# Which modulation chunks GpSimd sums in a two-layer mixer and MoE trunk, and when its residual rows are scaled

## Chip, cores and metric

The kernel runs on one core of a Trainium2 chip. The metric is the device time of one launch in microseconds. The kernel before takes 720.09 us, the median of three runs (717.9, 720.09 and 725.78).

## What is computed

The reference is a trunk of two layers on 256 tokens of width 1024. Each layer modulates its input with six vectors that come from one condition vector `c`, runs three token mixers (attention on selected keys, retention, mLSTM), and then a mixture of 16 experts of which two are taken for each token. Cut to what the change touches, it reads:

```python
c_act = silu(c)
for l in range(2):
    mod = c_act @ w_ada[l] + b_ada[l]            # w_ada[l]: 1024 x 6144
    sh_m, sc_m, g_m, sh_f, sc_f, g_f = split(mod, 6)
    h = x * (1 + sc_m) + sh_m
    mix = token_mixers(h, w_in[l], w_out[l], ...)   # key selection: top 64 of 256 scores
    x = layer_norm(ALPHA * x + (1 + g_m) * mix, ln_mix_g[l], ln_mix_b[l])
    h = x * (1 + sc_f) + sh_f
    y = moe_ffn(h, ...)
    x = layer_norm(ALPHA * x + (1 + g_f) * y, ln_ffn_g[l], ln_ffn_b[l])
```

## The kernel before

**Stages.** Each layer runs its mixers (the input projections in eight chunks, 0 to 7, then the output projection), then routing and the experts. Weights come through a ring of ten tiles of 512 KB that SyncE fills in the order of a written-out list; a tile is filled again when the engine that read it last is done. Every projection weight is split on chip into a high and a low part: ScalarE casts it (`A.copy` in `split`, L415), VectorE subtracts (L416), and TensorE multiplies three times (L434 to L436). So TensorE's projections are fed by ScalarE and VectorE, each of which takes its instructions in order.

**Modulation chunks.** `w_ada` is cut into 12 chunks of 512 columns for each layer, named (layer, chunk): 0 to 3 shift and scale of the mixers, 4 and 5 their gate, 6 to 9 shift and scale of the experts, 10 and 11 the experts' gate. A chunk is four tiles of the ring and is summed over 1024 rows in one of two ways:

- on TensorE (`ada`, L362, through `ada_half`, L349): 8 matmuls of 512 columns against the broadcast condition into PSUM, which the trace records as two passes each, a copy to SBUF (L364), then for a shift or scale four transposes (L404) and a small reduction on VectorE (L406), for a gate one summing matmul (L396). A gate's bias is added to the SBUF row by VectorE (L394), except where `ada_half` is told to add it by one more matmul (L353).
- on GpSimd (`ada_pool`, L370): ScalarE scales the eight half tiles by the condition (L210), GpSimd adds them up in seven additions of 128x512 (L380), and at the next call of `behind` TensorE sums over partitions with four one-column matmuls (L410).

`behind(n)` is called when the matmuls of projection chunk n have been written into the program. It first finishes chunks that GpSimd has summed, then starts those that the table `LATER` lists for n; `POOLED` names the ones that go to GpSimd.

**Key selection and softmax.** Scores of 256 keys (chunk 0's projection) go through eight rounds of MAX8 and MATCH_REPLACE on VectorE for each half of the tokens (L578 to L585) in the early part of each layer. The attention's softmax follows: VectorE masks and finds maxima (L623, L624), ScalarE takes the exponential, GpSimd multiplies by the reciprocal sums (L633), TensorE transposes (L636). The retention's rotation after chunk 5 uses GpSimd too (L528).

**Residual rows.** At the start of layer 1 the normalized rows `xn` (tile H) become the scaled residual `xres` (tile X) by eight GpSimd instructions (`affine_rows`, L463 and L464), for which two row tiles of 512 KB are loaded. The residual is used only after the output projection of the layer. In the convolution of the mLSTM a work tile `cvs` is taken from tag H.

The instructions of an engine stand in an order that a scheduler sets when the kernel is built, from the order of the code, its priorities and its waits.

## Time and profile before

| | |
|---|---|
| median of three runs | 720.09 us |
| the profiled execution | 720.78 us |
| its span, first to last instruction | 719.0 us |
| TensorE busy in it | 665.7 us (93%) |
| VectorE, ScalarE, GpSimd busy | 399.6, 281.2, 161.4 us |
| mean granted TensorE clock | 0.959 of 2.4 GHz |
| mixers of layer 0, then experts | 0 to about 217 us, 217 to 368 us |
| mixers of layer 1, then experts | 368 to about 556 us, 556 to 719 us |

The span is what the profiler saw between first and last instruction; the execution lasts 1.8 us longer. Busy shares are means over the whole span, so what a stage waits for is read from short windows of it: the busy time of each engine there, and beside it the granted clock, where 1.00 is 2.4 GHz and 0.50 is 1.2 GHz.

### The profile page before, as it was taken

How to read it: one execution, taken by the hardware profiler on the slowest of the kernel's cores; microseconds unless marked ns; L12 is line 12 of the kernel's file. 1: busy time of each engine (PE TensorE's matmuls, PEld its weight loads, DVE VectorE, ACT ScalarE, POOL GpSimd, SP SyncE). 2: the span in 40 equal slices, each digit the busy share in tenths (PEclk: the TensorE clock that was granted, in tenths of full speed). 3: DMA queues.
4: the chain of work that ended last, by engine and by line, in shares of the span. 5: the costliest groups of instructions: out<-in, count | busy, mean ns of one | idle time of the engine just before them, and what ended most of it. 6: DMA issues, size and time to landing. Idle time of an engine off the chain costs nothing. (4 is left out here: it accounts for less than half of the span.)

```text
span 719.0 us, 10379 instructions
## 1 busy us (share of the span) xinstructions
PE 665.7 (93%) x3638; PEld 410.1 (57%) x3638; DVE 399.6 (56%) x911; ACT 281.2 (39%) x583; POOL 161.4 (22%) x163
## 2 busy tenths in 40 slices
PE   5899799999998999989989999999999799999994
PEld 1567687865775433434338678894576644434431
DVE  5478987643765331244377999764547522234345
ACT  3346748344622222222246646853633221222231
POOL 3012943200003036120035513310000303612001
PEclk9999979999996999999997999999999699999998
DMA  8997773499996899999945773447998569999951
GB/s 305 407 377 240 253 261 96 145 342 410 411 359 252 288 322 364 357 406 410 383 142 183 242 244 114 138 153 253 402 326 257 194 237 326 347 350 407 406 190 58
DMA packets 57759, 204.18 MB, mean 284 GB/s; under 512 B 7336, under 2 KB 7464, under 8 KB 56422
## 3 DMA queue, kind: packets, MB, share of 16 engines
q1 hardware_dynamic: 55152, 198.49, 75.7%
q0 software_dynamic: 2112, 4.44, 1.6%
q8 instruction: 30, 0.49, 0.3%
q10 hardware_dynamic: 438, 0.54, 0.2%
q14 instruction: 27, 0.22, 0.1%
HBM read 202.15 MB, written 4.19 MB: 287 GB/s over the span
## 5 line engine op out<-in xcount | busy, mean ns | idle before, releaser
L416 DVE TENSOR_TENSOR sb_w<-sb_ring,sb_w 128x512 fp32r<-128x512 f32 (+1 forms) x156 | 109.8, 715 | 44.7 <-ACT sb_w L415 43.1
L415 ACT CAST sb_w<-sb_ring 128x512 fp32r<-128x512 f32 (+1 forms) x156 | 92.0, 608 | 82.4 <-PE ps_mm L435 49.1
L1205 PE MATMUL ps_s<-sb_ring,sb_S 128*64 128x512 f32 x424 | 113.8, 601 | 0.2 <-PEq L1114 0.2
L435 PE MATMUL ps_mm<-sb_w,sb_H 128*128 128x512 f32 (+2 forms) x224 | 80.7, 363 | 3.3 <-DVE sb_H L889 3.3
L434 PE MATMUL ps_mm<-sb_w,sb_H 128*128 128x512 f32 (+2 forms) x224 | 80.7, 368 | 2.4 <-ACT sb_w L415 1.7
L436 PE MATMUL ps_mm<-sb_w,sb_H 128*128 128x512 f32 (+2 forms) x224 | 75.6, 373 | 0.8 <-DVE sb_w L416 0.6
L1205 PEld LDWEIGHTS ps_s<-sb_ring,sb_S 128*64 128x64 f32 x424 | 32.3, 137 | 54.3 <-issue 48.1
L349 PE MATMUL ps_t<-sb_ring,cact 128*32 128x512 f32 x272 | 48.0, 621 | 7.2 <-DVE posf L296 6.2
L434 PEld LDWEIGHTS ps_mm<-sb_w,sb_H 128*128 128x128 f32 x224 | 43.7, 197 | 11.3 <-ACT sb_w L415 2.7
L435 PEld LDWEIGHTS ps_mm<-sb_w,sb_H 128*128 128x128 f32 x224 | 44.0, 197 | 9.1 <-DVE sb_H L889 4.0
L436 PEld LDWEIGHTS ps_mm<-sb_w,sb_H 128*128 128x128 f32 x224 | 42.3, 197 | 12.1 <-issue 3.8
L1104 DVE TENSOR_SCALAR sb_S<-ps_t,afffg,afffb 128x256 f32<-128x256 f32 x32 | 17.4, 543 | 51.7 <-ACT sb_S L210 51.7
L1096 PEld LDWEIGHTS ps_t<-sb_O,sb_H 128*128 128x128 f32 x256 | 33.1, 193 | 19.9 <-issue 12.2
L1253 PE MATMUL ps_t<-sb_P,sb_sg 128*64 128x512 f32 x152 | 42.0, 599 | 0.9 <-ACT sb_sg L1240 0.9
L210 ACT ACTIVATE sb_S<-ps_t,afffb,afffg 128x256 f32<-128x256 f32 x32 | 18.0, 563 | 59.1 <-PE ps_t L1096 59.0
L1096 PE MATMUL ps_t<-sb_O,sb_H 128*128 128x256 f32 x256 | 38.9, 297 | 2.0 <-DVE sb_O L1026 1.8
L435 PE MATMUL ps_mm<-sb_H,sb_w 128*128 128x256 f32 x128 | 38.1, 298 | 2.8 <-DVE sb_w L416 2.8
L434 PE MATMUL ps_mm<-sb_H,sb_w 128*128 128x256 f32 x128 | 37.9, 298 | 0.0
L436 PE MATMUL ps_mm<-sb_H,sb_w 128*128 128x256 f32 x128 | 37.9, 296 | 0.0
L1036 POOL MEMSET sb_X<- 128x2048 f32 x2 | 3.6, 1804 | 151.3 <-DVE sb_H L836 151.3
L633 POOL TENSOR_SCALAR sb_sg<-sb_sg,sm 128x128 f32<-128x128 f32 (+1 forms) x32 | 26.4, 842 | 47.1 <-DVE sm L630 24.9
L528 POOL TENSOR_TENSOR sb_rope<-sb_rope 128x256 f32<-128x256 f32 (+1 forms) x16 | 15.9, 992 | 89.1 <-DVE iwm L564 31.3
(369 smaller groups left out, 1214.2 us busy)
## 6 DMA issues: line engine op xcount, KB each, us to landing
sb_ring<-w_gu SPq DMA_DIRECT2D x106, 512.0 KB, 7.0
sb_ring<-w_ada SPq DMA_DIRECT2D x96, 512.0 KB, 7.1
sb_P<-w_dn SPq DMA_DIRECT2D x58, 512.0 KB, 9.7
sb_ring<-w_in SPq DMA_DIRECT2D x56, 512.0 KB, 6.0
sb_ring<-w_out SPq DMA_DIRECT2D x16, 512.0 KB, 10.1
sb_S<-w_gu SPq DMA_DIRECT2D x6, 1024.0 KB, 8.2
sb_row<-rows SPq DMA_DIRECT2D x8, 512.0 KB, 8.1
sb_w<-w_gu SPq DMA_DIRECT2D x12, 256.0 KB, 3.9
```

What stands on the lines that cost most here:

```text
L210: return A.activation(o, i, f, bias=bias, scale=scale)
L349: PE.matmul(pa[32 * g:32 * g + 32, :], cact[:, k:k + 1].to_broadcast([P, 32]), w[g // 2][:, (g % 2) * 512:(g % 2) * 512 + 512], start=(i = ...
L415: A.copy(hi, src)
L416: V.tensor_tensor(lo, src, hi.bitcast(F32), op=OP.subtract)
L434: PE.matmul(o, a[0], b[0], start=start, stop=False)
L435: PE.matmul(o, a[1], b[0], start=False, stop=False)
L436: return PE.matmul(o, a[0], b[1], start=False, stop=stop)
L633: G.tensor_scalar(sg[:, i * n:(i + 1) * n], sg[:, i * n:(i + 1) * n], sm[:, h:h + 1], None, op0=OP.mult)
L1096: last = PE.matmul(pt[:, j * 256:(j + 1) * 256], src[:, tt * D + k * P:tt * D + (k + 1) * P], oh[:, tt * D + q * 256:tt * D + (q + 1) * 25 ...
L1104: V.tensor_scalar(o, t, gp[:, k:k + 1], bp[:, k:k + 1], op0=OP.mult, op1=OP.add)
L1205: PE.matmul(pgu[s * 64:s * 64 + 64, :], xg[:, c0:c0 + 64], ws[s][k], start=(i == order[0] and k == 0), stop=(i == order[3] and k == 1), ti ...
L1253: PE.matmul(pyb[s * 64:s * 64 + 64, :], hdT[:, k, s * 64:s * 64 + 64], wd[s][k], start=(k == 0), stop=(k == 1), tile_position=(0, 64 * s))
```

## The change

Three things change together.

1. The tables. In layer 0, chunks (0,6) and (0,7), which GpSimd summed behind projection chunk 3, are summed on TensorE behind chunk 2; (0,5) moves from behind chunk 2 to behind chunk 1; (1,0) and (1,2), which TensorE summed behind chunk 6, are summed by GpSimd behind chunks 5 and 6. In layer 1, (1,6) and (1,7), which TensorE summed behind chunk 6, are summed by GpSimd behind chunks 5 and 6.
2. Gates that TensorE sums with `ada` get their bias by the extra matmul (L353): (0,4), (0,5) and (1,10).
3. The residual rows of layer 1 are scaled behind chunk 5, in place in `xn`, and issued after the last softmax multiplication of GpSimd, not at the layer's start; their loads move in the list from ahead of chunk 0 to ahead of chunk 6. The convolution's work tile is taken from tag X in layer 1.

In all, TensorE loses two chunks (16 matmuls of 512 columns and 8 transposes) and gets three bias matmuls and eight one-column matmuls more; GpSimd has 14 additions more; ScalarE has 16 scalings more and two copies fewer; VectorE loses three bias additions and two reductions.

```diff
@@ -48,11 +48,12 @@
 LATE_ROWS = (False, True)
 
 
-LATER = [{2: [(0, 5)], 6: [(0, 9), (1, 0), (1, 2)], 3: [(0, 6), (0, 7)], 5: [(0, 8)], 7: [(1, 3), (1, 1)], 1: [(0, 4)]}, {2: [(1, 5), (1, 8)], 6: [(1, 10), (1, 7), (1, 6)], 7: [(1, 9)]}]
+LATER = [{1: [(0, 4), (0, 5)], 2: [(0, 6), (0, 7)], 5: [(1, 0), (0, 8)], 6: [(1, 2), (0, 9)], 7: [(1, 3), (1, 1)]},
+         {2: [(1, 5), (1, 8)], 5: [(1, 6)], 6: [(1, 7), (1, 10)], 7: [(1, 9)]}]
 EARLY = [[], [(1, 4)]]
 LAST = [[(0, 10), (0, 11)], [(1, 11)]]
 
-POOLED = [(1, 5), (0, 6), (0, 7)]
+POOLED = [(1, 0), (1, 2), (1, 5), (1, 6), (1, 7)]
 
 SLOT = {"ring": 1024, "X": 2048, "H": 2048, "O": 2048, "S": 2048, "P": 1024,
         "w": 512, "rope": 512, "sg": 512, "e": 512, "a": 512, "h": 256, "g0": 1024, "g1": 1024, "row": 1024}
@@ -153,13 +154,13 @@
                     st.add(("in", l, n), chunk(l, n), which=(i,))
         for la, na in EARLY[l]:
             st.add(("ada", la, na), w_ada[la, na])
-        if l:
-            norm_rows(2 * l - 1)
         for n in range(8):
             if l or n > 1:
                 st.add(("in", l, n), chunk(l, n))
             for la, na in LATER[l].get(n, ()):
                 st.add(("ada", la, na), w_ada[la, na])
+            if l and n == 5:
+                norm_rows(2 * l - 1)
         norm_rows(2 * l)
         for n, which in ((0, (0, 1)), (1, (0, 1)), (0, (2,)), (1, (2,)), (0, (3,)), (1, (3,))):
             st.add(("out", l, n), w_out[l, n], which=which)
@@ -361,8 +362,9 @@
 
     def ada(l, n, tag="t"):
         a = sb("a")
-        (V.tensor_copy if n < 4 and l == 0 else A.copy)(a, ada_sums(l, n, tag))
-        modulation(l, n, a, quad, tag)
+        gate = n % 6 > 3
+        (V.tensor_copy if n < 4 and l == 0 else A.copy)(a, ada_sums(l, n, tag, gate))
+        modulation(l, n, a, quad, tag, gate)
 
     pending = []
 
@@ -505,6 +507,9 @@
             if l == 0 and n == 5:
                 with tc.issue_after(st.last.ins):
                     nc.sync.dma_start(xres, x_tok)
+            if l and n == 5:
+                with tc.issue_after(behind.soft.ins):
+                    affine_rows(xres, xres, 2 * l - 1)
             while pending:
                 modulation(*pending.pop(0), ones, "t")
             for la, na in LATER[l].get(n, ()):
@@ -630,7 +635,7 @@
                     V.reciprocal(sm[:, h0:h1], sm[:, h0:h1])
                     for i in range(per):
                         h = h0 + i
-                        G.tensor_scalar(sg[:, i * n:(i + 1) * n], sg[:, i * n:(i + 1) * n], sm[:, h:h + 1], None, op0=OP.mult)
+                        behind.soft = G.tensor_scalar(sg[:, i * n:(i + 1) * n], sg[:, i * n:(i + 1) * n], sm[:, h:h + 1], None, op0=OP.mult)
                     pt = ps("t")
                     for j in range(4):
                         PE.transpose(pt[:, j * P:(j + 1) * P], sg[:, j * P:(j + 1) * P], ident)
@@ -687,7 +692,7 @@
         for k, w in blocks(3):
             cols_part(k, wsplit(w), [pm[j // 2][:, (j % 2) * 256:(j % 2) * 256 + 256] for j in range(4)])
         behind(3)
-        cvs = sb("H").rearrange("p (i j t) -> p i j t", i=2, j=4)
+        cvs = sb("X" if l else "H").rearrange("p (i j t) -> p i j t", i=2, j=4)
         cv, sg = cvs[:, 0], cvs[:, 1]
         mq = sb("S")
         mqk = mq[:, 0:1024].rearrange("p (h t) -> p h t", h=4)
@@ -892,8 +897,8 @@
                 with tc.issue_after(moved.ins):
                     A.copy(a, sums)
                 modulation(la, na, a, quad, "t", True)
-            xres = sb("X")
-            affine_rows(xres, xn, 2 * l - 1)
+
+            xres = xn
 
         oT = projections(l, hT, inputs)
```

On GpSimd in layer 0, from the rotation ahead of the key selection (L528, L533 in the changed kernel) over the softmax (L633, L638) to the retention's rotation: before,

```order
L528 TENSOR_TENSOR sb_rope<-sb_rope 128x8x32 x4
L380 TENSOR_TENSOR sb_a<-sb_a,sb_ring 128x512 x14
L633 TENSOR_SCALAR sb_sg<-sb_sg,sm 128x128 x8
L633 TENSOR_SCALAR sb_sg<-sb_sg,sm 128x256 x8
L528 TENSOR_TENSOR sb_rope<-sb_rope 128x8x32 x2
```

and in the changed kernel:

```order
L533 TENSOR_TENSOR sb_rope<-sb_rope 128x8x32 x4
L638 TENSOR_SCALAR sb_sg<-sb_sg,sm 128x128 x8
L382 TENSOR_TENSOR sb_a<-sb_a,sb_ring 128x512
L638 TENSOR_SCALAR sb_sg<-sb_sg,sm 128x256 x2
L382 TENSOR_TENSOR sb_a<-sb_a,sb_ring 128x512 x3
L638 TENSOR_SCALAR sb_sg<-sb_sg,sm 128x256 x2
L382 TENSOR_TENSOR sb_a<-sb_a,sb_ring 128x512
L638 TENSOR_SCALAR sb_sg<-sb_sg,sm 128x256 x4
L382 TENSOR_TENSOR sb_a<-sb_a,sb_ring 128x512 x2
L533 TENSOR_TENSOR sb_rope<-sb_rope 128x8x32 x2
L382 TENSOR_TENSOR sb_a<-sb_a,sb_ring 128x512 x7
```

The 14 additions of modulation chunks (L380, L382) stood in one block ahead of the softmax; now seven stand between and behind the softmax multiplications and seven behind the rotation.

On GpSimd in layer 1, from the last attention rotation over the softmax to the retention's rotation (the last row with L528, L533) and the memset of the experts' stage: before,

```order
L528 TENSOR_TENSOR sb_rope<-sb_rope 128x8x32 x4
L633 TENSOR_SCALAR sb_sg<-sb_sg,sm 128x128 x8
L633 TENSOR_SCALAR sb_sg<-sb_sg,sm 128x256 x8
L528 TENSOR_TENSOR sb_rope<-sb_rope 128x8x32 x2
L1036 MEMSET sb_X 128x2048
L970 TENSOR_TENSOR sb_H<-sb_H 128x1024 x2
```

and in the changed kernel (L465 and L466 are the residual rows):

```order
L638 TENSOR_SCALAR sb_sg<-sb_sg,sm 128x256 x2
L382 TENSOR_TENSOR sb_a<-sb_a,sb_ring 128x512 x2
L638 TENSOR_SCALAR sb_sg<-sb_sg,sm 128x256 x4
L382 TENSOR_TENSOR sb_a<-sb_a,sb_ring 128x512 x3
L638 TENSOR_SCALAR sb_sg<-sb_sg,sm 128x256 x2
L465 TENSOR_TENSOR sb_H<-sb_H,sb_row 128x512 x4
L382 TENSOR_TENSOR sb_a<-sb_a,sb_ring 128x512
L466 TENSOR_TENSOR sb_H<-sb_H,sb_row 128x512 x2
L1041 MEMSET sb_X 128x2048
L466 TENSOR_TENSOR sb_H<-sb_H,sb_row 128x512 x2
L382 TENSOR_TENSOR sb_a<-sb_a,sb_ring 128x512
L533 TENSOR_TENSOR sb_rope<-sb_rope 128x8x32
```

Before the last softmax multiplications stand seven additions of (1,6) and three of (1,7), and between them and the rotation the residual rows, the memset and two more additions.

On ScalarE in layer 1 behind the projection of chunk 4, casts of chunk 5's weights (L415, L417) with softmax exponentials (L211, L212, the ones of `sb_sg`) and copies of its transposes (L641, L646): before,

```order
L415 CAST sb_w<-sb_ring 128x512
L211 ACTIVATE sb_sg,sm<-sb_sg,mx 128x256 x4
L210 ACTIVATE sb_e<-sb_e,ones 128x512
L210 ACTIVATE sb_H<-sb_H 128x1024
L415 CAST sb_w<-sb_ring 128x512
L641 COPY sb_P<-ps_t 128x2x256 x2
L415 CAST sb_w<-sb_ring 128x512 x4
L641 COPY sb_P<-ps_t 128x2x256
L415 CAST sb_w<-sb_ring 128x512
```

and in the changed kernel, where `sb_ring<-sb_ring,cact` and `sb_a<-sb_ring,cact` are scalings of chunk (1,7):

```order
L417 CAST sb_w<-sb_ring 128x512
L211 ACTIVATE sb_ring<-sb_ring,cact 128x512 x2
L211 ACTIVATE sb_X<-sb_X,ones 128x1024
L646 COPY sb_P<-ps_t 128x2x256
L212 ACTIVATE sb_sg,sm<-sb_sg,mx 128x256 x2
L211 ACTIVATE sb_ring<-sb_ring,cact 128x512 x2
L417 CAST sb_w<-sb_ring 128x512
L211 ACTIVATE sb_ring<-sb_ring,cact 128x512 x2
L646 COPY sb_P<-ps_t 128x2x256
L211 ACTIVATE sb_X<-sb_X 128x1024
L417 CAST sb_w<-sb_ring 128x512
L646 COPY sb_P<-ps_t 128x2x256
```

Six of the eight scalings of (1,7) stand here, among the casts of chunk 5 and on both sides of its last exponentials; the first two stand ahead of these rows.

## Rows read from the trace of the kernel before

**Rows 1.** Windows, 60 to 100 us: busy by engine, clock, DMA share.

```profile
76.00:80.00 4.00, 1.36 (x10) 1.32 (x10) 4.00 (x9) 4.00 (x8) 3.84 (x4) 0.95 0.84 337
80.00:84.00 4.00, 4.00 (x24) 3.96 (x23) 4.00 (x14) 1.97 (x4) 4.00 (x3) 0.63 0.61 177
...
88.00:92.00 4.00, 1.82 (x6) 1.16 (x4) 3.90 (x11) 2.05 (x5) 3.57 (x3) 0.73 0.94 334
92.00:96.00 4.00, 4.00 (x11) 2.63 (x11) 4.00 (x12) 0.88 (x4) 0.00 (x0) 0.50 0.91 342
96.00:100.00 4.00, 4.00 (x21) 4.00 (x20) 2.27 (x6) 1.48 (x6) 0.88 (x2) 0.50 0.73 223
sum 40.00, PE 35.01 PEld 28.59 DVE 37.07 ACT 25.13 POOL 23.87; mean PE 3.50 PEld 2.86 DVE 3.71 ACT 2.51 POOL 2.39
```

**Rows 2.** Timeline of GpSimd, 66 to 92 us: start, duration, instruction, count.

```profile
70.65 21.07 POOL L380 TENSOR_TENSOR sb_a<-sb_a,sb_ring 128x512 f32<-128x512 f32 x14
```

**Rows 3.** Timeline of VectorE, 68 to 94 us.

```profile
68.00 0.68 DVE L416 TENSOR_TENSOR sb_w<-sb_ring,sb_w 128x512 fp32r<-128x512 f32 x1
...
76.88 1.75 DVE L416 TENSOR_TENSOR sb_w<-sb_ring,sb_w 128x512 fp32r<-128x512 f32 x1
...
81.70 1.63 DVE L416 TENSOR_TENSOR sb_w<-sb_ring,sb_w 128x512 fp32r<-128x512 f32 x1
```

**Rows 4.** Waits of TensorE over the whole span: total, times, longest.

```profile
PE ps_mm L435 <- DVE sb_H L889: 3.3, 2, 1.8
...
PE ps_mm L435 <- DVE sb_w L416: 2.8, 2, 2.6
```

**Rows 5.** Windows of 4 us, 372 to 388 us, columns as in rows 1.

```profile
372.00:376.00 4.00, 1.99 (x11) 1.14 (x10) 3.92 (x5) 3.31 (x9) 4.00 (x3) 1.00 0.88 297
376.00:380.00 4.00, 2.83 (x10) 2.38 (x10) 4.00 (x5) 2.80 (x7) 4.00 (x4) 0.57 0.81 325
380.00:384.00 4.00, 3.24 (x12) 3.25 (x13) 4.00 (x5) 0.82 (x2) 3.33 (x3) 0.50 0.20 46
384.00:388.00 4.00, 4.00 (x21) 3.95 (x21) 3.37 (x9) 2.59 (x7) 0.00 (x0) 0.65 0.65 211
```

**Rows 6.** Timeline of GpSimd, 368 to 410 us.

```profile
371.86 5.66 POOL L463 TENSOR_TENSOR sb_X<-sb_H,sb_row 128x512 f32<-128x512 f32 x4 [0.32 <-DVE sb_H L1286]
377.49 5.84 POOL L464 TENSOR_TENSOR sb_X<-sb_X,sb_row 128x512 f32<-128x512 f32 x4
```

**Rows 7.** Timeline of VectorE, 371 to 392 us.

```profile
377.81 2.89 DVE L889 TENSOR_TENSOR sb_H<-sb_h,sb_H 128x256 fp32r<-128x256 f32 x2
...
384.81 0.41 DVE L889 TENSOR_TENSOR sb_H<-sb_h,sb_H 128x256 fp32r<-128x256 f32 x1
```

**Rows 8.** Windows of 4 us, 440 to 468 us, columns as in rows 1.

```profile
456.00:460.00 4.00, 4.00 (x20) 3.29 (x19) 1.78 (x5) 4.00 (x10) 1.82 (x2) 1.00 0.45 133
460.00:464.00 4.00, 3.57 (x20) 2.67 (x19) 1.52 (x4) 4.00 (x11) 3.41 (x4) 1.00 0.22 79
...
sum 28.00, PE 27.57 PEld 23.52 DVE 23.05 ACT 24.44 POOL 13.54; mean PE 3.94 PEld 3.36 DVE 3.29 ACT 3.49 POOL 1.93
```

**Rows 9.** Groups by line and shape, whole span: count, busy, mean ns, idle before.

```profile
L349 PE MATMUL ps_t<-sb_ring,cact 128*32 128x512 f32 x272 | 48.0, 621 | 7.2 <-DVE posf L296 6.2 <-DMA sb_ring<-w_ada 0.8
...
L210 ACT ACTIVATE sb_ring<-sb_ring,cact 128x512 f32<-128x512 f32 x21 | 14.0, 715 | 2.1 <-DMA sb_ring<-w_ada 2.1
...
L404 PE MATMUL ps_t<-ident,sb_a 128*128 128x128 f32 x56 | 8.8, 279 | 3.4 <-DVE sb_a L364 3.3
...
L353 PE MATMUL ps_mm<-rowz,ident 128*32 128x512 f32 x6 | 3.1, 592 | 0.0
```

**Rows 10.** Groups of TensorE by line, whole span.

```profile
L410 PE MATMUL ps_t<-ones,sb_a 128*128 128x1 f32 x16 | 2.0, 243 | 0.0
```

**Rows 11.** Windows of 20 us, 100 to 120 us, columns as in rows 1.

```profile
100.00:120.00 20.00, 20.00 (x125) 17.26 (x125) 13.81 (x31) 16.71 (x43) 8.35 (x12) 1.00 0.49 153
```

**Rows 12.** Timeline of GpSimd, 436 to 482 us.

```profile
475.42 1.59 POOL L528 TENSOR_TENSOR sb_rope<-sb_rope 128x256 f32<-128x256 f32 x1 [10.07 <-DVE rowz L661]
```

## Prediction

> **What bounds the kernel now.** I read the shares of busy time first, and then short windows, because a share of 93% for TensorE over the span says only that most stages are bound by TensorE and not where the other 7% lie. The windows show three kinds of place around the change.
>
> In layer 0's key selection TensorE is not the bound. From 60 to 100 us it is busy 35.0 of 40 us, while VectorE is busy 37.1 and full in nearly every window [rows 1]. Besides the 5.0 us without work, TensorE runs part of the stretch at its lower clock: it has only 1.36 us of work in 76 to 80, and the next window has a granted clock of 0.63; it has 1.82 in 88 to 92 and then 0.50 for two windows. A busy microsecond at clock c does c microseconds of full-speed work, so these windows lose 4.00 x 0.37 + 1.82 x 0.27 + 4.00 x 0.50 x 2 = 6.0 us more. The place owes 11.0 us in all to something that is not TensorE. GpSimd does 14 additions in one block there, 21.07 us [rows 2]. While it does, VectorE's 128x512 subtraction, which takes 0.68 us ahead of the block, takes 1.75 and 1.63 [rows 3]. The longest wait of TensorE for such a subtraction is 2.6 us [rows 4].
>
> The start of layer 1 is the second such place. From 372 to 384 GpSimd is nearly full, and TensorE is busy 1.99, 2.83 and 3.24 of 4 us, so 3.94 us are empty, and the clock goes to 0.57, 0.50 and 0.65 afterwards [rows 5], which loses 2.83 x 0.43 + 3.24 x 0.50 + 4.00 x 0.35 = 4.2 us. GpSimd's work is the eight residual instructions, 5.66 + 5.84 = 11.5 us [rows 6]. Two subtractions of VectorE take 2.89 us together at that time and 0.41 us each just behind it [rows 7], and TensorE waits 3.3 us for this line [rows 4].
>
> Elsewhere, in layer 1 from 440 to 468, TensorE is the bound (27.57 of 28 us). But ScalarE stands close behind it there: 24.44 of 28 us, and 4.00 of 4 in the windows from 456 to 464 [rows 8].
>
> **Layer 0, part by part.** The block of 14 additions leaves the key selection, so the stretched instructions go back to their short form. Two new chunks on TensorE fall into the same stage. One costs 16 passes and 4 transposes (two records each). Sixteen passes are 48.0 / 272 x 16 = 2.8 us, the transposes 8.8 / 14 = 0.6 us [rows 9], so two chunks bring 6.9 us, less the small matmuls of two sums (2.0 us for 16 records, so two chunks' worth [rows 10]): 4.9 us. Since 5.0 us stand empty there and as much of (1,0) and (1,2) leaves the TensorE-bound part later on, this work is free if it fits. What can be won is the 11.0 us. At the least nothing is won: VectorE's rounds of MAX8 are a chain of their own and could still end when they did. At the most all 11.0 us are. I take 6.0: VectorE gets back about a microsecond for each of some six struck instructions (1.75 - 0.68 = 1.07), TensorE's own work grows into the idle time, and part of the lower clock stays. Of the 16 scalings of 0.715 us that (1,0) and (1,2) put on ScalarE [rows 9], the eight of (1,0), 5.7 us, come in or behind 100 to 120 us, where ScalarE is busy 16.71 of 20 us and TensorE all 20 [rows 11]; (1,2) stands behind chunk 6. The 3.3 us of room and what follows take them, so I cost them at nothing, with 0 to 5.7 us for the case that casts wait behind them.
>
> The extra bias matmuls cost 3.1 / 3 = 1.0 us each [rows 9]. Two of three fall into the stage with idle time and replace the one-partition additions there; I take 1.2 us in all (0 to 3.1).
>
> **Layer 1, part by part.** Without the residual rows at its start, the subtractions stay short and GpSimd is empty. The 3.94 us of idle time and 4.2 us of lower clock can go, so 0 to 8.1 us; I take 4.0, because the transposes, casts and modulated copies of that start still go through ScalarE and VectorE in turn. The row loads that move are two of 512 KB; the DMA is far from full in both places (shares 0.20 to 0.88 here, and 0.45 to 0.22 around 460 [rows 5, 8]), so I cost them at nothing.
>
> (1,6) and (1,7) leave TensorE behind chunk 6, where nothing else bounds: two chunks less their small matmuls, 4.9 us (3.8 to 5.9 if the passes overlap more or less than the mean); I take 4.5.
>
> What layer 1 pays stands on ScalarE and GpSimd between 440 and 480. Sixteen scalings come in, 16 x 0.715 = 11.4 us, nearly all among the casts of chunks 4 and 5 and the softmax exponentials, as the order shows. ScalarE has 28.00 - 24.44 = 3.56 us free there; two scalings may go ahead of 440, so about 10.0 us want 3.56, and the last casts of chunk 5 come 6.5 us later. TensorE waits in its order for these casts. What it has in hand (the rest of chunk 4, the transposes) covers some 2 us: 4.5 us of wait. On GpSimd the last softmax multiplications stand behind three additions of (1,7), and the rotation after chunk 5 behind eight residual instructions, two additions and a memset. Before, GpSimd stood idle for 10.07 us ahead of that rotation [rows 12]; now it has 11.5 us of rows and some 3 us of additions there, so the rotation is perhaps 5 to 6 us late. TensorE's transposes of it stand behind other projection work; I take 1.0 us. Together 5.5 us, with bounds of 0 (TensorE has enough in hand) and 6.5 + 6 + 4.2 (one stage at the lower clock as in rows 5) = 16.7 us.
>
> The Trainium skill speaks against this part: "SBUF — State Buffer", section "Who interferes with whom", says that VectorE and GpSimd share a pair of ports that one instruction holds as a whole, and that a VectorE instruction with two inputs in SBUF is blocked by a GpSimd instruction that reads SBUF. The trace agrees: 1.75 against 0.68 us [rows 3] and 1.45 (2.89 / 2) against 0.41 us [rows 7]. By the rule every one of the 14 additions could block one such instruction, 14 x 1.07 = 15 us of VectorE where I leave room for some 5; the sum here would become about 713.0 + 10 = 723.
>
> That is too much by the rows: from 456 to 464 VectorE is busy only 3.3 of 8 us [rows 8], so what is late by some microseconds is caught up there, and only the first half of the additions falls ahead of that. I leave it inside the 5.5 us.
>
> **The sum.** From the profiled execution's 720.8 us: -6.0 (key selection) -4.0 (start of layer 1) -4.5 (two chunks) +1.2 (biases) +5.5 (ScalarE and GpSimd in layer 1) = 713.0 us. The profiled execution lies 0.7 us above the median, which I neglect. A measurement of this kernel can tell about 1% (7.2 us) from no change, so the forecast lies almost on the border between faster (below 712.9) and the same (to 727.3).
>
> **Rivals.**
> (a) The wait in layer 1 doesn't come, because TensorE has chunk 4 and the transposes in hand while ScalarE catches up: 713.0 - 5.5 = 707.5. For it: TensorE is busy 27.57 of 28 us there, so work is queued ahead of it. Against it: ScalarE is already full for eight of these us.
> (b) The key selection is VectorE's own chain. MAX8 and MATCH_REPLACE aren't what was stretched, TensorE has two chunks more ahead of it, and the 6.0 us aren't won: 719.0. For it: VectorE is busy 4.00 of 4 us also from 92 to 96, when GpSimd does nothing [rows 1]. Against it: six struck instructions by a microsecond stand in that chain.
> (c) Slower: ScalarE's order in layer 1. A scaling waits for its tile of (1,7), whose slot in the ring is free only after casts of chunk 5; behind it stand the next casts, and the last exponentials, and behind these the multiplications, rows and rotation on GpSimd. If nothing is hidden, TensorE waits the full 10.0 us of scalings, the 6 us of the rotation, and runs two stages at the lower clock (2 x 4.2), 24 us in place of 5.5: 731.5. It decides for slower from 713.0 - 5.5 + 20 = 727.5 on, so from 20 us of lost time. For it: all these queues are strictly in order. Against it: two full stalls have to add up, and none of rows 4 is longer than 2.6 us.
> That the change does not do what it says can be excluded by the order: the blocks have moved as the tables say.
>
> **Chances.** The forecast 0.36, with its own range 708 to 718, half of it on either side of the border. (a) 0.24, faster. (b) 0.22, the same. (c) 0.18, slower. So faster is 0.24 + 0.18 = 0.42, the same 0.22 + 0.18 = 0.40, slower 0.18. For the range I leave out the lowest part of (a) and most of (c): 704.5 to 725.
>
> **What would show it.** In the changed kernel's profile: the subtractions (L418) at 68 to 92 us near 0.68 and the windows from 76 to 100 with TensorE above 3.5 us and a clock near 1.00; the window from 372 to 384 with GpSimd near zero and no clock at 0.50; behind chunk 6 in layer 1 no passes of (1,6) and (1,7); ScalarE at 4.00 from 440 to 470 and TensorE's waits for its casts (L417) or for GpSimd (L638, L533) above 1 us. The prediction is wrong if the clock in the key selection stays at 0.50 and TensorE still idles there, or if the stretch from 436 to 500 is longer by more than 10 us or not at all.

## The result, and the profile after

The changed kernel is slower, by a little over 1%. It takes 729.78 us (median of four runs, 726.64 to 731.72) against 719.31 us for the kernel before (four runs); the ratio is 1.0134 with a 95% interval of 1.0096 to 1.0172. Here and below the ratio takes in every run, so it can differ a little from that of the medians. The forecast was 713.0 us, with a range of 704.5 to 725.0. The profiled execution took 729.49 us.

The page of the changed kernel, first part (busy time, share of the span, instructions):

```profile
span 727.6 us, 10347 instructions
...
PE 666.3 (92%) x3620; PEld 407.3 (56%) x3620; DVE 401.6 (55%) x906; ACT 289.8 (40%) x597; POOL 187.5 (26%) x177
```

The span grew by 8.6 us. TensorE's busy time did not fall although two chunks left it, its mean granted clock even rose from 0.959 to 0.964, and GpSimd has 26 us more. So TensorE stands idle 8.0 us longer, and these sums do not say where.

The windows of the changed kernel that answer to [rows 1], the key selection of layer 0, and one behind it:

```profile
76.00:80.00 4.00, 3.64 (x31) 2.68 (x23) 4.00 (x10) 1.21 (x2) 1.11 (x1) 1.00 1.02 384
80.00:84.00 4.00, 4.00 (x37) 4.00 (x36) 3.97 (x15) 1.90 (x4) 0.00 (x0) 1.00 1.00 395
...
92.00:96.00 4.00, 4.00 (x29) 3.53 (x28) 2.31 (x6) 4.00 (x14) 3.26 (x5) 1.00 0.47 136
96.00:100.00 4.00, 4.00 (x34) 3.95 (x34) 3.19 (x8) 4.00 (x11) 4.00 (x6) 1.00 0.00 0
...
104.00:108.00 4.00, 1.70 (x12) 1.50 (x12) 4.00 (x9) 3.76 (x10) 1.76 (x2) 1.00 0.54 179
108.00:112.00 4.00, 3.21 (x17) 3.14 (x17) 2.53 (x9) 2.55 (x6) 4.00 (x4) 0.66 0.41 121
```

The key selection went as hoped: TensorE idles 0.36 us in 76 to 80 where it idled 2.64, and from 80 to 100 it is full at 1.00. Worked out from windows of 20 us (length less busy times clock), 60 to 100 us lose 0.7 us where they lost 11.0. But 104 to 108, among the softmax and the sums of (1,0), is new: 1.70 us of work and then a clock of 0.66; 100 to 120 lose 5.1 us where before they lost none. From 40 to 60, where chunks now stand closer together, 1.5 us are lost that were not before.

The windows that answer to [rows 5], the start of layer 1:

```profile
372.00:376.00 4.00, 2.90 (x17) 1.26 (x12) 3.42 (x7) 3.74 (x8) 0.47 (x2) 1.00 0.82 273
376.00:380.00 4.00, 4.00 (x27) 3.83 (x28) 3.94 (x11) 3.88 (x10) 0.00 (x0) 1.00 0.99 370
380.00:384.00 4.00, 4.00 (x27) 3.85 (x26) 3.23 (x8) 3.90 (x9) 0.00 (x0) 1.00 0.89 313
```

GpSimd is nearly empty, and the clock stays at 1.00. This part did what was forecast, and more.

The windows around those of [rows 8], layer 1's softmax and the end of chunk 5:

```profile
456.00:460.00 4.00, 3.79 (x19) 2.78 (x17) 0.77 (x1) 4.00 (x9) 3.42 (x3) 1.00 0.79 274
460.00:464.00 4.00, 2.08 (x10) 1.42 (x10) 0.86 (x2) 4.00 (x10) 3.30 (x4) 1.00 0.45 150
464.00:468.00 4.00, 1.86 (x9) 0.93 (x8) 2.99 (x2) 3.53 (x7) 4.00 (x4) 0.96 0.42 137
468.00:472.00 4.00, 3.77 (x13) 3.13 (x14) 4.00 (x5) 1.24 (x2) 4.00 (x3) 0.61 0.26 72
```

Here it breaks. TensorE has 2.08 and 1.86 us of work in two windows running and then a clock of 0.61, while ScalarE is full to 464 and GpSimd full from 464 on. GpSimd's timeline (start, duration, instruction, count, idle before) says what it does there:

```profile
455.79 1.30 POOL L382 TENSOR_TENSOR sb_a<-sb_a,sb_ring 128x512 f32<-128x512 f32 x1 [0.15 <-ACT sb_ring L211]
457.59 2.65 POOL L382 TENSOR_TENSOR sb_a<-sb_a,sb_ring 128x512 f32<-128x512 f32 x2 [0.51 <-ACT sb_ring L211]
460.94 1.83 POOL L638 TENSOR_SCALAR sb_sg<-sb_sg,sm 128x256 f32<-128x256 f32 x2 [0.70 <-DVE sm L635]
462.74 6.58 POOL L465 TENSOR_TENSOR sb_H<-sb_H,sb_row 128x512 f32<-128x512 f32 x4
469.28 1.72 POOL L382 TENSOR_TENSOR sb_a<-sb_a,sb_ring 128x512 f32<-128x512 f32 x1
470.96 6.12 POOL L466 TENSOR_TENSOR sb_H<-sb_H,sb_row 128x512 f32<-128x512 f32 x2
...
484.65 1.11 POOL L533 TENSOR_TENSOR sb_rope<-sb_rope 128x256 f32<-128x256 f32 x1 [0.36 <-DVE rowz L666]
```

The last softmax multiplications start at 460.94, behind three additions of (1,7), and behind them stand the residual rows: 6.58 us for four, then 6.12 us for two. The rotation (L533), which GpSimd began at 475.42 before [rows 12], begins at 484.65, though layer 1's index scores came 6.1 us earlier. GpSimd had been free for 0.36 us by then: the last thing that it waited for was VectorE (`rowz`, L666), whose instructions ahead of that are lengthened too, as the last section shows.

To see where the lead is won and lost I took the same instructions (marks) from both timelines, as they start:

| mark | before | changed, against before |
|---|---|---|
| last softmax transpose, layer 0 | 131.7 | -14.8 |
| last head norm, layer 0 | 187.7 | -0.1 |
| first expert matmul, layer 0 | 236.3 | -3.5 |
| first transpose of layer 1 | 372.1 | +0.9 |
| first index scores, layer 1 | 404.8 | -6.1 |
| last transpose of the rotation, layer 1 | 481.2 | +7.8 |
| last head norm, layer 1 | 530.8 | +8.3 |
| last instruction | 719.0 | +8.6 |

The first mark flatters: TensorE has 91 projection matmuls fewer behind it there than before (342 records of L436 to L438 against 433 of L434 to L436) and does them later. By the last head norm it has done as many, and nothing of the lead is left; where layer 1 begins, 0.9 us are lost. The start of layer 1 wins 7.0; the stretch from the index scores to the rotation loses 13.9; from there to the last head norm 0.5 more are lost, although the passes of (1,6) and (1,7) are gone from it; and behind it 0.3. In all: 0.9 - 7.0 + 13.9 + 0.5 + 0.3 = 8.6.

### The profile page after: what moved, and what is told of

Read it like the earlier page. It is cut to its first block, busy times and chain, and to the rows that moved or that the text cites. A ratio compares the mean times of both kernels' runs of the same rounds, so it can differ in the third digit from the quotient of the medians.

```text
span 727.6 us, 10347 instructions
## 1 busy us (share of the span) xinstructions
PE 666.3 (92%) x3620; PEld 407.3 (56%) x3620; DVE 401.6 (55%) x906; ACT 289.8 (40%) x597; POOL 187.5 (26%) x177
## 5 line engine op out<-in xcount | busy, mean ns | idle before, releaser
L418 DVE TENSOR_TENSOR sb_w<-sb_ring,sb_w 128x512 fp32r<-128x512 f32 (+1 forms) x156 | 116.5, 756 | 67.6 <-ACT sb_w L417 65.0
L417 ACT CAST sb_w<-sb_ring 128x512 fp32r<-128x512 f32 (+1 forms) x156 | 92.9, 611 | 87.2 <-PE ps_mm L437 59.2
L1210 PE MATMUL ps_s<-sb_ring,sb_S 128*64 128x512 f32 x424 | 117.4, 605 | 0.2 <-PEq L1119 0.2
L436 PE MATMUL ps_mm<-sb_w,sb_H 128*128 128x512 f32 (+2 forms) x224 | 80.6, 367 | 1.8 <-ACT sb_w L417 1.1
L438 PE MATMUL ps_mm<-sb_w,sb_H 128*128 128x512 f32 (+2 forms) x224 | 75.0, 367 | 4.7 <-DVE sb_w L418 4.7
L382 POOL TENSOR_TENSOR sb_a<-sb_a,sb_ring 128x512 f32<-128x512 f32 x35 | 52.1, 1490 | 23.6 <-ACT sb_ring L211 22.4
L438 PEld LDWEIGHTS ps_mm<-sb_w,sb_H 128*128 128x128 f32 x224 | 41.1, 192 | 15.2 <-DVE sb_w L418 7.7
L436 PEld LDWEIGHTS ps_mm<-sb_w,sb_H 128*128 128x128 f32 x224 | 42.7, 192 | 11.9 <-ACT sb_w L417 3.1
L350 PE MATMUL ps_t<-sb_ring,cact 128*32 128x512 f32 x240 | 40.0, 620 | 7.6 <-DVE cact L221 6.2
L437 PEld LDWEIGHTS ps_mm<-sb_w,sb_H 128*128 128x128 f32 x224 | 43.1, 192 | 6.4 <-issue 0.9
L211 ACT ACTIVATE sb_S<-ps_t,afffb,afffg 128x256 f32<-128x256 f32 x32 | 18.1, 565 | 61.9 <-PE ps_t L1101 56.8
L533 POOL TENSOR_TENSOR sb_rope<-sb_rope 128x256 f32<-128x256 f32 (+1 forms) x16 | 16.1, 1005 | 88.8 <-DVE iwm L569 30.7
L438 PE MATMUL ps_mm<-sb_H,sb_w 128*128 128x256 f32 x128 | 37.3, 293 | 0.0
L437 PE MATMUL ps_mm<-sb_H,sb_w 128*128 128x256 f32 x128 | 37.0, 290 | 0.4 <-DVE sb_w L418 0.4
L436 PE MATMUL ps_mm<-sb_H,sb_w 128*128 128x256 f32 x128 | 37.1, 294 | 0.0
L211 ACT ACTIVATE sb_rope<-ps_s 128x256 f32<-128x256 f32 x16 | 6.1, 384 | 65.2 <-PE ps_s L1210 65.2
```

The lines of the kernel that those rows point to most:

```text
L211: return A.activation(o, i, f, bias=bias, scale=scale)
L350: PE.matmul(pa[32 * g:32 * g + 32, :], cact[:, k:k + 1].to_broadcast([P, 32]), w[g // 2][:, (g % 2) * 512:(g % 2) * 512 + 512], start=(i = ...
L382: G.tensor_tensor(a, a, q, op=OP.add)
L417: A.copy(hi, src)
L418: V.tensor_tensor(lo, src, hi.bitcast(F32), op=OP.subtract)
L436: PE.matmul(o, a[0], b[0], start=start, stop=False)
```

## The experiments

All edits are against the kernel before unless another is named. Each run has its own interval against runs of the kernel before on its chip.

**Each part alone.** Run rows_only has part 3 of the change, l0_only and l1_only its tables of layer 0 and of layer 1, bias_only its part 2, each with the hunks shown in the change. `POOLED` becomes:

```diff
-POOLED = [(1, 5), (0, 6), (0, 7)]
+POOLED = [(1, 5), (1, 0), (1, 2)]                    # l0_only
+POOLED = [(1, 5), (0, 6), (0, 7), (1, 6), (1, 7)]    # l1_only
```

> The kernel before with only the residual rows moved behind chunk 5 (part 3), tables and biases as before. Theory A (the rows at the start of layer 1 cost some 7 us there, and GpSimd's 10 idle us ahead of the retention's rotation hide them at the new place): 713 to 715 us, the start of layer 1 about 7 us shorter and the stretch from 460 to 490 not more than 2 us longer. Theory B (GpSimd's order there is what costs the 14 us that the changed kernel loses between 430 and 490): the gain is given back behind chunk 5, 719 to 727 us, the retention's rotation 6 us late and TensorE waiting for it.

> The kernel before with only layer 0's table changed ((0,6), (0,7) on TensorE behind chunk 2, (0,5) earlier, (1,0), (1,2) on GpSimd). Theory A (the key selection's idle time and lower clock are worth about 9 us and the sums of (1,0) among the softmax cost about 5): 714 to 717 us. Theory B (the sums of (1,0) cost as much as the key selection gains): 719 to 723 us.

> The kernel before with only layer 1's table changed ((1,6), (1,7) on GpSimd behind chunks 5 and 6). Theory A (the 16 scalings and 14 additions among softmax and casts are what costs in layer 1): 725 to 732 us. Theory B (it is the residual rows behind the softmax that cost, and the sums are hidden): 716 to 720 us, as two chunks of TensorE's passes, 4.5 us, are saved.

> The kernel before with only the bias of (0,4), (0,5) and (1,10) by an extra matmul in place of VectorE's addition. All theories: 719 to 722 us, within what can be told; more than 723 would say that the order around the key selection turns on it.

Measured: rows_only 716.12 us, ratio 0.9941 (0.9908 to 0.9974); l0_only 726.17 us, 1.0102 (1.0070 to 1.0135); l1_only 732.65 us, 1.0192 (1.0142 to 1.0242); bias_only 722.74 us, 1.0065 (1.0040 to 1.0091). rows_only lies between its two theories, l0_only above both, l1_only just above theory A, and bias_only just above the range that all theories gave. Of the parts only the rows are a gain, and layer 1's table alone costs as much as the whole change or more (the intervals overlap). The ratios less one add to 3.0%, more than twice the change's 1.3%: the parts overlap. The same marks for these and later runs, from their timelines, each against the kernel before:

| run | experts 0 | layer 1 | index scores 1 | rotation 1 | head norm 1 | end |
|---|---|---|---|---|---|---|
| changed kernel | -3.5 | +0.9 | -6.1 | +7.8 | +8.3 | +8.6 |
| rows_only | -2.0 | -0.3 | -7.2 | -1.4 | -3.5 | -4.0 |
| rows7 | -2.4 | -2.4 | -9.4 | -9.4 | -6.0 | -6.4 |
| l1_only | -2.1 | -2.0 | -2.4 | +6.9 | +8.1 | +10.4 |
| l1_noadd | 0.0 | +0.1 | -0.6 | +6.6 | +6.8 | +6.8 |
| l1_noscale | -4.9 | -1.5 | -2.1 | +3.8 | +5.1 | +5.4 |
| l1_neither | -1.6 | -1.6 | -2.1 | -2.0 | -3.7 | -2.1 |
| l1_later | -4.0 | -2.3 | -3.3 | -3.3 | -1.7 | +0.2 |
| no_pass | -1.9 | -1.8 | -2.9 | -2.9 | -4.4 | -3.0 |
| l0_only | -0.3 | +4.3 | +3.8 | +3.8 | +3.7 | +4.5 |
| l0_sel | -6.6 | -1.7 | -3.0 | -3.1 | -0.2 | +0.1 |
| l0_pool | +0.7 | +8.8 | +7.5 | +7.4 | +7.2 | +7.6 |
| bias_only | -6.6 | -0.9 | -1.6 | -1.6 | +0.3 | +1.3 |

From one column to the next one reads what a stretch won or lost. Each row is one trace. The eight kernels that have layer 0 as it was come to its experts 0.0 to 4.9 us earlier than before and take up to 3.4 us longer in them, so in layer 0 only larger steps are read. From the index scores to the rotation the eight kernels in this table that leave GpSimd and ScalarE there as they were differ by 0.1 us at most, so that stretch can be read closely.

**Scalings, additions or the ring: layer 1's sums.** Three kernels take l1_only apart. l1_noadd leaves out the 14 additions of (1,6) and (1,7), l1_noscale the 16 scalings, and l1_neither both and the closing matmuls, so that only the tiles are loaded, at their new place (its code is the hunk shown for no_pass below).

```diff
                 act(o, q, AF.Copy, scale=cact[:, k:k + 1])
-                if k:
+                if k and (l, n) not in ((1, 6), (1, 7)):
                     G.tensor_tensor(a, a, q, op=OP.add)
```

```diff
+                if (l, n) in ((1, 6), (1, 7)):
+                    if k == 1:
+                        G.tensor_tensor(a, w[:, 0:512], q, op=OP.add)
+                    elif k:
+                        G.tensor_tensor(a, a, q, op=OP.add)
+                    continue
                 act(o, q, AF.Copy, scale=cact[:, k:k + 1])
```

> The kernel with layer 1's new table alone (run l1_only, 732.65 us), but the 14 GpSimd additions of (1,6) and (1,7) are left out; the 16 ScalarE scalings stay, so the two sums are of one half tile of eight. Theory A (ScalarE's scalings among the casts and exponentials cost): still 727 to 733 us, the casts of chunk 5 as late as in l1_only. Theory B (GpSimd's order, the softmax multiplications behind additions that wait for tiles, and the struck VectorE instructions cost): 713 to 720 us.

> The same kernel, but the 16 ScalarE scalings of (1,6) and (1,7) are left out and the 14 additions stay, on unscaled tiles. Theory A (scalings): 714 to 720 us. Theory B (GpSimd's order and the shared port): 726 to 733 us. If both of these runs lie between 720 and 727, each has its part.

> Layer 1's new table alone, but of (1,6) and (1,7) only the tiles are loaded, at their new place in the list; scalings, additions and the matmuls that end the sums are left out (shift and scale are the bias alone). Theory A (the engines' queues cost: ScalarE's scalings and GpSimd's additions each hold what stands behind them): from the index scores to the retention's rotation no longer than before, total 715 to 720 us as in no_pass. Theory B (the new place of eight tiles in the ring of ten makes the projections' weights late, whoever reads the tiles): that stretch 4 to 7 us longer, total 722 to 727 us.

Measured: l1_noadd 726.8 us, 1.0107 (1.0044 to 1.0169); l1_noscale 728.5 us, 1.0154 (1.0074 to 1.0234); l1_neither 718.17 us, 0.9972 (0.9938 to 1.0005). l1_neither is as theory A has it; l1_noadd lies just below its theory A (ScalarE's scalings), l1_noscale within its theory B (GpSimd's order and the port), so both have their part. From the index scores to the rotation l1_only loses 9.3 us, l1_noadd 7.2, l1_noscale 5.9, l1_neither 0.1. So loading the tiles at their new place costs nothing as long as nobody works on them, and neither ScalarE's scalings nor GpSimd's additions alone are the cause: either is enough for most of it, and together they cost little more than one. The tiles still play a part: from 425 to 490 the scalings of l1_noadd wait 6.4 us for theirs (`w_ada`), with casts behind them in order, while no cast waits for its own weights. ScalarE's side shows in l1_noadd, casts of chunk 5 (L415) and scalings (`cact`) in its timeline there:

```profile
462.04 0.61 ACT L415 CAST sb_w<-sb_ring 128x512 fp32r<-128x512 f32 x1
462.55 0.73 ACT L210 ACTIVATE sb_ring<-sb_ring,cact 128x512 f32<-128x512 f32 x1
...
464.16 0.72 ACT L210 ACTIVATE sb_ring<-sb_ring,cact 128x512 f32<-128x512 f32 x1
...
465.24 1.34 ACT L210 ACTIVATE sb_ring<-sb_ring,cact 128x512 f32<-128x512 f32 x2
...
468.03 0.61 ACT L415 CAST sb_w<-sb_ring 128x512 fp32r<-128x512 f32 x1
```

Two casts stand 6 us apart, with four scalings among other work between them, and TensorE in the windows of that run:

```profile
464.00:468.00 4.00, 1.24 (x6) 0.40 (x4) 0.61 (x2) 4.00 (x8) 1.83 (x2) 1.00 0.73 233
468.00:472.00 4.00, 3.30 (x9) 2.33 (x10) 2.00 (x4) 4.00 (x9) 0.00 (x0) 0.58 0.55 196
```

It has 1.24 us of work in the first, then waits 1.8 us for a cast, up to 468.7, and has a clock of 0.58 in the second. GpSimd's side shows in l1_noscale, in the waits of its additions from 425 to 490 (total, times, longest):

```profile
POOL sb_a L380 <- DMA sb_ring<-w_ada: 5.6, 2, 5.3
```

An addition waits 5.3 us for a tile, up to 432, and from 435.2 four stand in a block of 6.11 us. TensorE's idle time follows, with 2.63 and 2.74 us of work in 440 to 444 and 444 to 448: it waits 1.4 us for a mask of VectorE, and 1.5 us in three waits for softmax multiplications that stand behind additions. The additions act in two ways, by their place in GpSimd's order and on VectorE: beside that block VectorE's scaling of the maxima, an instruction of 128x4 (L625, L631 in that kernel), takes 1.26 and 1.25 us, where it takes 0.16 at 455.5, with GpSimd idle, and the exponentials behind it wait up to 4.2 us (2.9 before). No run here tells the two apart. In l1_neither the windows of l1_noadd's loss are whole:

```profile
464.00:468.00 4.00, 4.00 (x26) 3.52 (x26) 3.69 (x8) 2.79 (x7) 0.00 (x0) 1.00 0.89 311
468.00:472.00 4.00, 4.00 (x36) 4.00 (x35) 3.97 (x7) 1.71 (x3) 0.00 (x0) 1.00 0.66 246
```

**What two chunks are worth on TensorE.** no_pass leaves TensorE's passes, transposes and copies of (1,6) and (1,7) out of the kernel before (shift and scale are the bias alone); l1_later sums them on GpSimd one chunk later (`POOLED` as in l1_only).

```diff
+                if (la, na) in ((1, 6), (1, 7)):
+                    for i in range(4):
+                        st.get(("ada", la, na, i))
+                    V.tensor_copy(modc[la][:, 2:4, 2 * (na - 6):2 * (na - 6) + 2], bada[:, la, na - 2, :].rearrange("p (s k) -> p s k", s=2))
-                if (la, na) in POOLED:
+                elif (la, na) in POOLED:
```

```diff
-{2: [(1, 5), (1, 8)], 6: [(1, 10), (1, 7), (1, 6)], 7: [(1, 9)]}
+{2: [(1, 5), (1, 8)], 6: [(1, 10), (1, 6)], 7: [(1, 7), (1, 9)]}
```

> The kernel before with TensorE's passes, transposes and copies of (1,6) and (1,7) left out (their tiles are still loaded; the shift and scale of layer 1's experts are the bias alone). Theory A (behind chunk 6 TensorE waits for the chain of the retention and the head norms, and the passes only fill it): 716 to 721 us, and more idle time or lower clock from 500 to 560. Theory B (TensorE bounds there, as the prediction's -4.5 us has it): 713 to 716 us with the mixers of layer 1 shorter by 4 to 5 us.

> Layer 1's sums of (1,6) and (1,7) on GpSimd, but started one chunk later each (behind chunks 6 and 7), all else as before, so that they stand behind the softmax. Theory A (what costs is where they stand, among softmax and casts of chunk 5; the two chunks are worth 4.5 us of TensorE): 714 to 717 us. Theory B (a sum on GpSimd costs more than it saves wherever it stands): 721 to 730 us.

Measured: no_pass 716.69 us, 0.9982 (0.9956 to 1.0008); l1_later 720.9 us, 1.0011 (0.9976 to 1.0045). no_pass falls in theory A's range, l1_later between its two. With nothing in their place, not even the one-column matmuls of a sum on GpSimd, 6.9 us of work leave TensorE (2 x 2.8 for the passes, 2 x 0.6 for the transposes, as in the prediction), and that wins no more than 0.4%. From the index scores to the last head norm no_pass wins 1.5 us; the passes had filled time in which TensorE waits. In l1_later the sums stand behind the rotation, and GpSimd takes them up at 488:

```profile
488.39 2.99 POOL L380 TENSOR_TENSOR sb_a<-sb_a,sb_ring 128x512 f32<-128x512 f32 x2 [11.65 <-ACT sb_a L210]
492.66 12.55 POOL L380 TENSOR_TENSOR sb_a<-sb_a,sb_ring 128x512 f32<-128x512 f32 x9 [1.27 <-ACT sb_ring L210]
```

No softmax multiplication waits behind them there, and from the index scores to the rotation nothing is lost; but the 1.6 us up to the last head norm and the 1.9 us behind it take back what was won by then. Windows of no_pass:

```profile
500.00:520.00 20.00, 18.11 (x102) 11.47 (x99) 9.07 (x23) 9.35 (x17) 0.00 (x0) 0.86 0.68 225
520.00:540.00 20.00, 19.22 (x140) 15.40 (x139) 8.90 (x13) 8.78 (x15) 0.00 (x0) 0.97 0.79 270
540.00:560.00 20.00, 16.45 (x80) 12.78 (x79) 14.42 (x21) 5.54 (x11) 4.65 (x3) 0.88 0.83 274
```

and of the kernel before:

```profile
500.00:520.00 20.00, 19.66 (x116) 12.16 (x114) 8.88 (x20) 10.15 (x18) 0.00 (x0) 1.00 1.02 402
520.00:540.00 20.00, 18.75 (x141) 14.71 (x141) 10.12 (x23) 8.52 (x15) 0.00 (x0) 1.00 0.93 324
540.00:560.00 20.00, 16.96 (x80) 12.50 (x79) 14.40 (x24) 6.12 (x12) 1.93 (x2) 1.00 0.84 265
```

Busy times clock is 15.6, 18.6 and 14.5 us in no_pass against 19.7, 18.8 and 17.0, in sum 6.8 us less in the same 60 us: what the passes leave behind is idle time and lower clock, while the retention and the head norms go through VectorE, ScalarE and TensorE by turns.

**The rows at another place.** rows7 is rows_only with `n == 7` for `n == 5` in both places of part 3.

> Run rows_only (716.12 us) with the residual rows behind chunk 7 in place of chunk 5, so that they stand behind the retention's rotation on GpSimd. Theory A (in rows_only the 7 us won at the start of layer 1 are cut to 3.5 by the rotation that stands behind the rows): 711 to 713.5 us, the rotation's transposes as early as the start of layer 1. Theory B (what is lost comes from the row loads or the tile that the convolution takes): 715 to 718 us.

Measured: 715.16 us, 0.9932 (0.9892 to 0.9971), the best of all kernels run, though its interval overlaps that of rows_only. The time lies in theory B's range, the marks are those of theory A: the rotation comes 9.4 us early where rows_only has 1.4, so it is the rows ahead of the rotation that cost there. Some 3 us of the lead are lost behind it, up to the head norms. GpSimd's rows in rows_only:

```profile
458.09 8.51 POOL L463 TENSOR_TENSOR sb_H<-sb_H,sb_row 128x512 f32<-128x512 f32 x4
...
468.31 7.49 POOL L464 TENSOR_TENSOR sb_H<-sb_H,sb_row 128x512 f32<-128x512 f32 x4
```

and in rows7:

```profile
498.60 5.92 POOL L463 TENSOR_TENSOR sb_H<-sb_H,sb_row 128x512 f32<-128x512 f32 x4 [29.22 <-DMA sb_row<-rows]
504.47 6.36 POOL L464 TENSOR_TENSOR sb_H<-sb_H,sb_row 128x512 f32<-128x512 f32 x4
```

Behind chunk 5 the eight take 16.0 us, behind chunk 7 12.3.

**Layer 0's two halves.** l0_sel has only (0,5) to (0,7) of the new table, l0_pool only (1,0) and (1,2); `POOLED` goes with them.

```diff
-{2: [(0, 5)], 6: [(0, 9), (1, 0), (1, 2)], 3: [(0, 6), (0, 7)], 5: [(0, 8)], 7: [(1, 3), (1, 1)], 1: [(0, 4)]}
+{1: [(0, 4), (0, 5)], 2: [(0, 6), (0, 7)], 5: [(0, 8)], 6: [(0, 9), (1, 0), (1, 2)], 7: [(1, 3), (1, 1)]}
```

```diff
-{2: [(0, 5)], 6: [(0, 9), (1, 0), (1, 2)], 3: [(0, 6), (0, 7)], 5: [(0, 8)], 7: [(1, 3), (1, 1)], 1: [(0, 4)]}
+{2: [(0, 5)], 5: [(1, 0), (0, 8)], 6: [(1, 2), (0, 9)], 3: [(0, 6), (0, 7)], 7: [(1, 3), (1, 1)], 1: [(0, 4)]}
```

> The kernel before with only the first half of layer 0's new table: (0,6), (0,7) on TensorE behind chunk 2, (0,5) behind chunk 1; (1,0), (1,2) stay on TensorE behind chunk 6. TensorE so has two chunks, 4.9 us, more to do than before. Theory A (the key selection's 11 us of idle time and lower clock are worth the 9 us that its windows show, and what costs in l0_only is the sums of (1,0) and (1,2)): 711 to 716 us. Theory B (what is won in the key selection is lost again behind it, to TensorE's own work and to the experts' loads): 718 to 724 us.

> The kernel before with only the second half: (1,0), (1,2) on GpSimd behind chunks 5 and 6; (0,6), (0,7) stay on GpSimd in the key selection. TensorE has 4.9 us less to do. Theory A (the sums of (1,0) among softmax and casts cost some 9 us there, as in layer 1): 722 to 730 us. Theory B (they are hidden, and the key selection's new order costs): 712 to 718 us.

Measured: l0_sel 720.06 us, 1.0009 (0.9979 to 1.0039); l0_pool 727.99 us, 1.0126 (1.0079 to 1.0174). In l0_sel, as in theory B, the key selection's gain is there (6.6 us at the first expert matmul, with two chunks more on TensorE), and then the experts of layer 0 take 4.9 us longer. Their weights are not late: the last windows of that stage in l0_sel

```profile
348.00:352.00 4.00, 1.91 (x8) 0.50 (x4) 2.64 (x6) 2.58 (x5) 0.00 (x0) 1.00 1.02 402
352.00:356.00 4.00, 4.00 (x12) 2.46 (x14) 0.67 (x2) 0.00 (x0) 0.00 (x0) 0.57 0.85 335
356.00:360.00 4.00, 2.46 (x12) 0.83 (x10) 2.36 (x4) 1.93 (x4) 0.00 (x0) 1.00 0.00 1
```

show the DMA done at 356, where before it is busy past 360, and still TensorE idles, 2.1 us of it for a cast (L415), and falls to 0.57. l0_pool comes to the experts 0.7 us late although TensorE has 4.9 us less to do ahead of them, so some 5.6 us are lost there, and 8.1 more in the experts: theory A had its time right and only part of its place. Over all 17 runs and the changed kernel, the experts of layer 0 take 4.4 to 8.1 us longer in the ten kernels in which layer 0's table or biases differ, and 0.0 to 3.4 us longer in the eight others. In the ten, 36 to 40 of TensorE's 614 matmuls within that stage stand in another order than before, in the eight none, though no code of the stage was touched. That the order is the cause was not tried by itself, and late weights are excluded by the windows for l0_sel alone: in bias_only, whose experts start 6.6 us earlier, the DMA is still at 0.81 from 356 to 360.

**One part undone, and two combinations.** no_l1, no_l0 and no_pool0 are the changed kernel with layer 1's table, layer 0's table, or (1,0) and (1,2) alone put back; rows7_sel and rows7_bias are rows7 with l0_sel's table or with the biases on TensorE.

> The changed kernel with layer 1's table put back ((1,6), (1,7) on TensorE behind chunk 6). Theory A (layer 1's sums cost some 11 us in the changed kernel too, as alone): 715 to 721 us. Theory B (with the residual rows behind chunk 5 the rows are what costs there): 725 to 730 us.

> The changed kernel with layer 0's table put back. Theory A (layer 0's table costs some 6 us in the changed kernel too, as alone, though its key selection is shorter): 720 to 726 us. Theory B (layer 0's part is a gain and all the loss is layer 1's): 729 to 735 us.

> The changed kernel with (1,0), (1,2) back on TensorE behind chunk 6; (0,6), (0,7) stay on TensorE in the key selection. Theory A (the sums of (1,0), (1,2) cost 6 to 9 us, as l0_pool alone): 720 to 725 us. Theory B (they are hidden here): 728 to 734 us, since TensorE has two chunks more.

> Run rows7 (715.16 us) with the table of l0_sel. Theory A (the gains of both add): 705 to 711 us. Theory B (layer 0's gain is lost behind it): 714 to 719 us.

> The kernel before with the residual rows behind chunk 7 and the biases of (0,4), (0,5), (1,10) on TensorE. Theory A (the biases cost 3 us because the experts of layer 0 stand in another order behind them): 716 to 720 us. Theory B (run bias_only's 3 us were chance): 712 to 716 us.

Measured: no_l1 720.45 us, 1.0025 (0.9997 to 1.0053); no_l0 728.25 us, 1.0094 (1.0056 to 1.0131); no_pool0 725.96 us, 1.0085 (1.0051 to 1.0119); rows7_sel 715.82 us, 0.9960 (0.9929 to 0.9992); rows7_bias 717.27 us, 0.9971 (0.9942 to 1.0000). no_l1 and rows7_bias fall in theory A's range, rows7_sel in theory B's, no_l0 and no_pool0 between theirs. Layer 1's table is 1.1 of the changed kernel's 1.3%. Layer 0's table is 0.4% in it, less than alone, and (1,0) and (1,2) are 0.5%, both with intervals that overlap, so their share there stays open. Neither combination beats rows7.

## Why the prediction was wrong, point by point

- **The key selection, -6.0 us.** The idle time and lower clock of 11.0 us fell to 0.7, more than was taken, but the block of additions was not the whole cause. In bias_only, which keeps 13 of the 14 additions in one block at the same place,

```profile
71.16 18.36 POOL L381 TENSOR_TENSOR sb_a<-sb_a,sb_ring 128x512 f32<-128x512 f32 x13 [1.26 <-ACT sb_a L210]
```

  60 to 100 us lose 4.6 us and the clock stays at 1.00 (no_l0, the same: 4.6); with the block moved and the additions of the biases left on VectorE (l0_sel) they lose 0.5. The step that failed is what stands behind: the scalings of (1,0), "so I cost them at nothing", took 5.1 us back in the softmax, within the stated 0 to 5.7 (without (1,0) and (1,2), in l0_sel and in no_pool0, 100 to 120 lose nothing), and no term stood for the experts of layer 0, which took 4.4 us more for a cause that stays open. With the 1.5 us of 40 to 60, +0.9 us stands at layer 1's start, where with the biases -4.8 was forecast.
- **The start of layer 1, -4.0 us.** Right, and 7.0 us in size: from the layer's first transpose to its index scores the eight kernels with late rows win 6.9 to 7.1 us, nearly all of the bound of 8.1.
- **Two chunks off TensorE, -4.5 us.** Failed at "behind chunk 6, where nothing else bounds". no_pass shows some 1.5 us, and in the changed kernel the stretch from the rotation to the last head norm is 0.5 us longer without the passes.
- **The biases, +1.2 us.** bias_only measured +3.1 us by the medians (0.65% by the ratio, some 4.7), at or above the upper end of the stated 0 to 3.1, and not as a price of matmuls: its experts start 6.6 us earlier and then take 5.7 us longer.
- **ScalarE and GpSimd in layer 1, +5.5 us.** The place was right, the term mis-sized, and it is the largest miss: 13.9 us, inside the bound of 16.7. The rows alone cost 5.8 us of it (rows_only) and the sums 9.3 (l1_only). The 4.5 us for late casts measured 7.2 (l1_noadd). GpSimd's additions among the softmax multiplications had no price and cost 5.9 by themselves (l1_noscale). The "1.0 us" for the rotation stands against 5.8 for the rows. From 430 to 490 TensorE of the changed kernel waits 3.2 us for VectorE's subtractions (L418), 2.1 for a softmax multiplication, 1.9 for the rotation and 0.9 for a cast.
- **The rivals.** (c), slower by the order of ScalarE and GpSimd in layer 1, had the place; that its 731.5 us lie 1.7 us above the measured 729.8 is luck. Its 24 us of loss in layer 1 measured 13.9, and the other 10 came from gains that it kept in the sum and that were not there: the two chunks, and the key selection as it reaches layer 1. Two full stalls did not add up, as was held against it; the losses are many short waits, and TensorE's longest for a softmax multiplication is 2.6 us, as its row of waits over the whole span says:

```profile
PE ps_t L641 <- POOL sb_sg L638: 4.8, 2, 2.6
```

(b) was wrong about the key selection itself, and near the truth for what reaches layer 1.

In the prediction's terms: forecast -4.8 - 4.0 - 4.5 + 5.5 = -7.8 us, measured 0.9 - 7.0 + 0.5 + 13.9 + 0.3 = +8.6. One reading there is off without harm: a transpose leaves one record and not two (56 records for 14 chunks), and the sum used the 0.6 us that a chunk's records take.

The Trainium skill's rule on the shared port ("SBUF — State Buffer", section "Who interferes with whom") was weighed for the 14 additions and left inside the 5.5 us. The trace agrees with it in both directions: a 128x512 subtraction of 0.67 us took 1.76 and two took 3.05 at 466 to 471, and GpSimd's additions of rows there took up to 3.06 each.

l1_noadd, which has no additions to block anything, still loses 7.2 us, so for the scalings this block is not needed. For the rest it was set aside too soon: the eight residual instructions were not counted as blocking. Between 466 and 485 in the changed kernel six entries of VectorE's timeline take 7.3 us more than the same lines in the kernel before (the longest are shown in the last section), and the rotation was released by the last of them, 0.36 us after GpSimd was free. How much of the rows' 5.8 us and of the additions' 5.9 is this, and how much GpSimd's order, no run here separates.

## What to carry to other kernels

Work taken off the busiest engine is worth only what a run without that work wins; where a chain through several engines follows, that work may be filling gaps, and its removal leaves idle time at a lower clock. Work given to a half-idle engine is priced by what stands behind it in that engine's order, by whom that feeds, and by what it does to other engines meanwhile: here scalings among casts, and additions among softmax multiplications, were each enough for most of the loss. A gain in one stage is followed by the same marks to the end before it is counted, with an eye on whether as much work stands ahead of the mark in both kernels; it can be given back in a stage whose code nobody touched.
